# The low part of k in the attention scores, held per head in both halves of a tile

## The chip, the cores and the metric

The program runs on one core of a Trainium2 chip. A core has TensorE (PE in the profile; its weight loads are listed apart as PEld), VectorE (DVE), ScalarE (ACT), GpSimd (POOL), and SyncE (SP), whose queue issues nearly all the DMAs here. The metric is the device time of one execution in microseconds (us). On this kernel a measurement can tell a change of about 0.2% from none.

## The reference, cut to what matters

Two transformer blocks follow each other on one sequence of 512 tokens with 1024 features. Each has an attention with 8 heads. In block 1 a head has 64 dimensions; in block 2 a head has two score maps of 64 dimensions each, whose softmaxes are subtracted:

```
scores = jnp.einsum('bcqhd,bckhd->bhcqk', q, kb).astype(jnp.float32) * scale
scores = scores + bias[None, :, None]
probs = jax.nn.softmax(scores, axis=-1).astype(v.dtype)
...
s = jnp.einsum('bqhid,bkhid->bihqk', qblk, kn)
s = jnp.where(allowed, s + bias, neg)
p = jax.nn.softmax(s, axis=-1)
a = p[:, 0] - lam * p[:, 1]
```

Around the attentions stand the projections, a state-space mixer (block 1), a pooling mixer and gates (block 2), output projections and two feed-forwards. The score products are a small part of the matrix work, but they are all that the change touches.

## The kernel before, in words

Matrix products run on a reduced fp32 format (fp32r). To keep the accuracy, each operand is split into a high and a low part, and three products are added: high by high, high by low, low by high. In the dense products this is `mm3` (lines 168 to 170) and `mm3s` (lines 173 to 175): three products of 128 rows by 512 columns into one PSUM bank. The weights come from HBM in 172 units of 512 KB on SP's queue (line 137), are split by ACT (line 156) and DVE or POOL (line 157), and one unit feeds 24 products.

The scores use a trick, since a head has only 64 dimensions and a tile has 128 rows. `stack_q` makes for a head pair (block 1) or for the two maps of a head (block 2) two tiles, `qa` for e = 0 and `qb` for e = 1: 64 rows with the high part of q and 64 rows with its low part. `stack_k` makes `ka` and `kb` with the high part of k in both halves, so that one product of 128 rows (line 379) gives high by high and low by high at once. The missing high by low is a second product (line 382). For it there is one tile `kl`, which holds the low part of k of both heads as the subtraction leaves it: rows 0 to 63 for e = 0 and rows 64 to 127 for e = 1. So this product takes 64 rows of `qs[e]` and 64 rows of `kl`. The copies between halves are DMAs from SBUF to SBUF on SP's queue (lines 359, 360, 369, 370), 128 KB each.

`scores` runs over four blocks of 128 queries. Block i needs 256, 256, 384 and 512 key columns. For each it takes a PSUM bank of the `ax` pool (4 banks, handed out in turn) per e, and yields; then DVE takes the row maxima out of the bank (`row_max`, line 343), which frees it. Block 1 calls `scores` for one e at a time (`a1_first`), so line 379 and line 382 alternate, and a stack serves two heads. Block 2 calls it for e = 0 and 1 together (`a2_first`): two products of line 379, then two of line 382; after i = 2 it yields to dense work, and i = 3 comes one dense step later. After the scores come the exponentials (ACT, line 351), in block 2 the joining of the maps (POOL line 1250, DVE line 1251), the transposes of the probabilities on PE (line 390) and their copies (lines 394, 396).

PE's order is the order of the program: `drive` deals out dense products and side work in turn. The order on the other engines and on SP's queue is set by a scheduler at build time, from a simulation and the data's dependencies. Tiles for the stacks come from `RB`, a few tiles of its own and then the shared arena `RA`, first in, first out; `RB.room(n)` asks whether n are free before the next head's stack is made (`a2_prep`, in block 2 about 15 us ahead of the scores that need it).

Of the kernel before, what the change touches and what calls it, by code (L numbers as in the profile page):

```python
# [9 lines left out]
F32 = mybir.dt.float32  # L10
F32R = mybir.dt.float32r
I32 = mybir.dt.int32
AF = mybir.ActivationFunctionType
ALU = mybir.AluOpType
# [42 lines left out]
class Arena:  # L57
# [9 lines left out]
    def take(self, n):  # L67
        return [self.get() for _ in range(n)]
# [22 lines left out]
def mixer_kernel(ctx, tc, xT, xN, wst, wfa, wfb, wdt, wgrp, rbt, par, con, frow, out):  # L91
    nc = tc.nc
    V, S, G, PE = nc.vector, nc.scalar, nc.gpsimd, nc.tensor
# [13 lines left out]
    def ax_bank():  # L107
        return ps_ax.tile([128, T], F32, tag="ax", name="ax")
# [10 lines left out]
    def C(name):  # L119
        a, b = _CON[name]  # L120
        return con_sb[:, a:b]
# [185 lines left out]
    RA = Arena(base, 32, F32R, "r")  # L307
# [33 lines left out]
    def row_max(i, b, bias, s, mx):  # L341
        n = 128 * (i + 1)
        V.tensor_tensor_reduce(out=s[:, SOFF[i]:SOFF[i] + n], in0=b[:, 0:n],
                               in1=bias[:, (3 - i) * 128:512], scale=1.0, scalar=-3.0e38,
                               op0=ALU.add, op1=ALU.max, accum_out=mx[:, i:i + 1])

    def exp_rows(s, mx, nm, Z):
        V.tensor_scalar(out=nm, in0=mx, scalar1=-1.0, scalar2=None, op0=ALU.mult)  # L348
        for i in range(NT):
            n = 128 * (i + 1)  # L350
            S.activation(out=s[:, SOFF[i]:SOFF[i] + n], in_=s[:, SOFF[i]:SOFF[i] + n], func=AF.Exp,  # L351
                         bias=nm[:, i:i + 1], accum_out=Z[:, i:i + 1])

    def stack_q(qf, take, put, eng):
        qa, qb, ql = take(3)
        S.activation(out=qa, in_=qf, func=AF.Copy)
        S.activation(out=qb[64:128, :], in_=qf[64:128, :], func=AF.Copy)
        eng.tensor_tensor(out=ql, in0=qf, in1=qa.bitcast(F32), op=ALU.subtract)
        nc.sync.dma_start(out=qb.bitcast(F32)[0:64, :], in_=ql.bitcast(F32)[64:128, :])
        nc.sync.dma_start(out=qa.bitcast(F32)[64:128, :], in_=ql.bitcast(F32)[0:64, :])  # L360
        put(ql)
        return qa, qb

    def stack_k(kf, take, eng):
        ka, kb, kl = take(3)
        S.activation(out=ka, in_=kf, func=AF.Copy)
        S.activation(out=kb[64:128, :], in_=kf[64:128, :], func=AF.Copy)
        eng.tensor_tensor(out=kl, in0=kf, in1=ka.bitcast(F32), op=ALU.subtract)
        nc.sync.dma_start(out=kb.bitcast(F32)[0:64, :], in_=kb.bitcast(F32)[64:128, :])
        nc.sync.dma_start(out=ka.bitcast(F32)[64:128, :], in_=ka.bitcast(F32)[0:64, :])  # L370
        return (ka, kb), kl

    def scores(qs, ks, kl, heads):
        for i in range(NT):
            n = max(256, 128 * (i + 1))
            q0 = i * 128
            bs = [ax_bank() for _ in heads]
            for b, e in zip(bs, heads):
                PE.matmul(b[:, 0:n], lhsT=qs[e][:, q0:q0 + 128], rhs=ks[e][:, 0:n], start=True, stop=False)  # L379
            for b, e in zip(bs, heads):  # L380
                r0, r1 = e * 64, e * 64 + 64
                PE.matmul(b[:, 0:n], lhsT=qs[e][r0:r1, q0:q0 + 128], rhs=kl[r0:r1, 0:n], start=False, stop=True)  # L382
            yield i, bs

    def probs_T(s, arena, flip):
# [11 lines left out]
            res.append(t)  # L397
        return res

    # first block: mixer  # L400
    with ExitStack() as ph:
        fa_p = ph.enter_context(tc.tile_pool(name="m1f", bufs=1))
        s_p = ph.enter_context(tc.tile_pool(name="m1s", bufs=2))
        c_p = ph.enter_context(tc.tile_pool(name="m1c", bufs=1))
        FA = Arena(fa_p, 28, F32, "f")
        RB = Both(Arena(fa_p, 2, F32R, "fx"), RA)
        lw = {}

        nc.sync.dma_start(out=par_sb[:, 0:8], in_=par[:, 0:8])
# [242 lines left out]
        def qk_evac(m, b):  # L652
            t, kind = divmod(m, 2)
            f = FA.get()
            if kind == 0:
                V.scalar_tensor_tensor(out=f, in0=b, scalar=0.125, in1=lw["rb1"], op0=ALU.mult, op1=ALU.mult)
            else:
                V.tensor_tensor(out=f, in0=b, in1=lw["rb1"], op=ALU.mult)
            qk[t, kind] = stack_k(f, RB.take, G) if kind else stack_q(f, RB.take, RB.put, G)
            FA.put(f)  # L660
# [23 lines left out]
        def a1_first(hh):  # L684
            t, e = divmod(hh, 2)
            if (t, 1) not in qk:
                while (t, 1) not in qk:
                    yield False
                for _ in range(4):
                    yield True  # L690
            bias = FA.get()
            nc.sync.dma_start(out=bias, in_=rbt[hh])
            G.memset(bias[0:64, 448:512], -1.0e30)
            qs, (ks, kl) = qk[t, 0], qk[t, 1]
            s = s_p.tile([128, 1280], F32, tag="s", name="s")
            mx, nm, Z, rz = (sm.tile([128, NT], F32, tag=g, name=g) for g in ("mx", "nm", "Z", "rz"))
            for i, bs in scores(qs, ks, kl, (e,)):
                row_max(i, bs[0], bias, s, mx)
            FA.put(bias)
            exp_rows(s, mx, nm, Z)  # L700
            V.reciprocal(out=rz, in_=Z)
            if e == 1:
                RB.put(*qs, *ks, kl)
            at[hh] = (s, rz)
            yield True

# [33 lines left out]
        def att_side():  # L740
            while len(vt) < NT:
                yield False
            yield from pipeline3(range(H1), a1_first, a1_second, a1_third, 0)
            FA.put(*vt)
            yield True
            att_T(3)
            ready.add("att")
            yield True
# [85 lines left out]
        RA.put(*sch)  # L834
        RA.put(*scl)

    # feed forward
    def feed_forward(fh, fl, xside, w2, eps, name, done):
        with ExitStack() as ph:
            f_p = ph.enter_context(tc.tile_pool(name=name + "f", bufs=1))  # L840
# [194 lines left out]

    feed_forward(fh, fl, xside, wfa, 1e-5, "a", done1)

    # second block: mixer
    with ExitStack() as ph:
        fa_p = ph.enter_context(tc.tile_pool(name="m2f", bufs=1))  # L1040
        s_p = ph.enter_context(tc.tile_pool(name="m2s", bufs=3))
# [6 lines left out]
        r1, r2, rr, r1s = (c_p.tile([128, NT], F32, name=n) for n in ("r1", "r2", "rr", "r1s"))  # L1048
# [95 lines left out]
        vt, qkT, osl = {}, {}, {}  # L1144
# [62 lines left out]
        stk = {}  # L1207
        RB = Both(RY, RA)

        def a2_prep(hh):  # L1210
            qf, kf = qkT.pop(("q", hh)), qkT.pop(("k", hh))
            ks, kl = stack_k(kf, RB.take, V)
            qs = stack_q(qf, RB.take, RB.put, G)
            FA.put(qf, kf)
            stk[hh] = (qs, ks, kl)

        def a2_first(hh):
            if hh not in stk:
                while ("k", hh) not in qkT or ("q", hh) not in qkT or not RB.room(6):
                    yield False  # L1220
                a2_prep(hh)
                for _ in range(3):
                    yield True
            qs, ks, kl = stk.pop(hh)
            bias = FA.get()
            G.tensor_scalar(out=bias, in0=C("dist"), scalar1=-(2.0 ** -(hh + 1)), scalar2=1.0, op0=ALU.mult,
                            op1=ALU.mult)
            ss, rzs, mxs = [], [], []
            for i2 in range(2):
                ss.append(s_p.tile([128, 1280], F32, tag="s", name="s"))  # L1230
                mxs.append(sm.tile([128, NT], F32, tag="mx", name="mx"))
            for i, bs in scores(qs, ks, kl, (0, 1)):
                for i2 in range(2):
                    row_max(i, bs[i2], bias, ss[i2], mxs[i2])
                if i == 2:
                    yield True
            RB.put(*qs, *ks, kl)
            for i2 in range(2):
                nm, Z, rz = (sm.tile([128, NT], F32, tag=g, name=g) for g in ("nm", "Z", "rz"))
                exp_rows(ss[i2], mxs[i2], nm, Z)  # L1240
                V.reciprocal(out=rz, in_=Z)
                rzs.append(rz)
            FA.put(bias)
            if ("k", hh + 1) in qkT and ("q", hh + 1) in qkT and RB.room(6):
                a2_prep(hh + 1)
            V.tensor_scalar(out=rzs[1], in0=rzs[1], scalar1=lam, scalar2=None, op0=ALU.mult)
            for i in range(NT):
                n = 128 * (i + 1)
                a, b = ss[0][:, SOFF[i]:SOFF[i] + n], ss[1][:, SOFF[i]:SOFF[i] + n]
                G.tensor_scalar(out=b, in0=b, scalar1=rzs[1][:, i:i + 1], scalar2=1.0, op0=ALU.mult, op1=ALU.mult)  # L1250
                V.scalar_tensor_tensor(out=a, in0=a, scalar=rzs[0][:, i:i + 1], in1=b, op0=ALU.mult, op1=ALU.add)  # L1251
            hd[hh] = ss[0]
            yield True
# [25 lines left out]
        def att2_side():  # L1279
            yield from pipeline3(range(H2), a2_first, a2_second, a2_third, 2)  # L1280
# [214 lines left out]
```

## Time and profile before

| | us |
|---|---|
| median of 3 runs | 1467.81 (1467.41 to 1470.63) |
| span of the profiled execution, first to last instruction | 1468.4 |
| PE busy in it | 1445.3 (98%) |
| DVE busy | 1023.9 (70%) |
| ACT busy | 659.9 (45%) |
| POOL busy | 284.5 (19%) |

The profile gives of the profiled execution its span, and tells of no time around it; the span is 0.6 us over the median of the timed runs. The granted clock of PE is 0.995 of full speed on average and 1.00 in both attention stretches. Block 1's scores lie between 164 and 284 us, block 2's between 803 and 1007 us. A matmul's row in the timeline gives its start and how long it took in all; since matmuls overlap in the array, what one costs PE is the step from its start to the start of the next. `64*128` in a row is the part of the array that it uses: 64 rows by 128 columns.

### The profile page before, as it was taken

Reading aid. Unit: us, or ns where it says so; the run is one execution under the profiler, and the core shown is the slowest. Engines: PE = TensorE matmul, PEld = TensorE weight load, DVE = VectorE, ACT = ScalarE, POOL = GpSimd, SP = SyncE. Lnnn points to the kernel's source line nnn. Section 1 sums busy time; section 2 is a strip of 40 time slices with the busy share of each in tenths; the row PEclk is TensorE's granted clock in tenths of the full one; section 3 lists DMA queues with packets and bytes.
Section 4 is the critical chain, followed back from the end, with each engine's and each line's share of the span. In section 5 each row is a group of like instructions: output and inputs, shape, how many; then the busy total and the mean of one; then the engine's idle time right before and its main releaser. Section 6 shows DMA issues by size and latency. Waiting matters only on the chain.

```text
span 1468.4 us, 17898 instructions
## 1 busy us (share of the span) xinstructions
PE 1445.3 (98%) x6683; PEld 1171.2 (80%) x6683; DVE 1023.9 (70%) x1761; ACT 659.9 (45%) x1108; POOL 284.5 (19%) x264
## 2 busy tenths in 40 slices
PE   8979999999999999999999999999999999999998
PEld 5867777888888888888878778778888888888887
DVE  7885654573887867778684675767654878768676
ACT  5433433443554535345534636554323544445452
POOL 4664720000001010102163342322110000010101
PEclk9989999999999999999999999999999999999999
DMA  7211322222524142420223323222233523241401
GB/s 251 87 48 60 115 65 73 72 73 86 202 71 144 47 156 70 144 86 30 79 86 108 101 77 94 80 88 73 72 100 94 207 78 124 61 152 46 158 29 58
DMA packets 43526, 141.17 MB, mean 96 GB/s; under 512 B 5296, under 2 KB 5552, under 8 KB 43440
## 3 DMA queue, kind: packets, MB, share of 16 engines
q1 hardware_dynamic: 43440, 140.04, 29.8%
q8 instruction: 52, 0.85, 0.2%
q14 instruction: 34, 0.28, 0.1%
HBM read 131.63 MB, written 2.10 MB: 91 GB/s over the span
## 4 chain that ended last, share of the span: by engine, by line
PE 87%; DVE 7%; POOL 3%; issue 2%; ACT 1%; DMA 0%; SPq 0%; POOLq 0%; ACTq 0%; DVEq 0%
PE mm L168 13%; PE mm L169 12%; PE mm L170 12%; PE mm L173 11%; PE mm L174 11%; PE mm L175 11%; PE ax L175 2%; PE ax L174 2%; PE ax L173 2%; PE ax L379 1%; PE ax L382 1%; DVE wl L157 1%; PE ax L1263 1%; PE ax L721 1%; DVE s L1251 1%
## 5 line engine op out<-in xcount | busy, mean ns | idle before, releaser
L168 PE MATMUL mm<-r,wh 128*128 128x512 f32 x928 | 371.1, 400 | 0.0
L169 PE MATMUL mm<-r,wh 128*128 128x512 f32 x928 | 363.0, 391 | 1.2 <-DVE r L294 1.0
L170 PE MATMUL mm<-r,wl 128*128 128x512 f32 x928 | 362.8, 391 | 1.1 <-DVE wl L157 1.1
L156 ACT ACTIVATE wh<-wr 128x1024 fp32r<-128x1024 f32 (+1 forms) x173 | 182.4, 1054 | 388.3 <-PE mm L169 146.4
L157 DVE TENSOR_TENSOR wl<-wr,wh 128x1024 fp32r<-128x1024 f32 (+1 forms) x171 | 229.1, 1340 | 114.4 <-ACT wh L156 114.0
L173 PE MATMUL mm<-wh,r 128*128 128x512 f32 x512 | 207.2, 405 | 0.0
L168 PEld LDWEIGHTS mm<-r,wh 128*128 128x128 f32 x928 | 175.3, 189 | 39.8 <-issue 4.3
L169 PEld LDWEIGHTS mm<-r,wh 128*128 128x128 f32 x928 | 175.2, 189 | 39.5 <-DVE r L294 2.0
L170 PEld LDWEIGHTS mm<-r,wl 128*128 128x128 f32 x928 | 174.9, 189 | 38.6 <-DVE wl L157 1.5
L175 PE MATMUL mm<-wh,r 128*128 128x512 f32 x512 | 200.0, 391 | 0.0
L174 PE MATMUL mm<-wl,r 128*128 128x512 f32 x512 | 199.7, 390 | 0.3 <-DVE wl L157 0.3
L299 POOL TENSOR_TENSOR vl<-u,vh 128x512 fp32r<-128x512 f32 x36 | 47.8, 1328 | 758.2 <-ACT vh L298 757.8
L173 PEld LDWEIGHTS mm<-wh,r 128*128 128x128 f32 x512 | 96.2, 188 | 23.1 <-issue 4.4
L174 PEld LDWEIGHTS mm<-wl,r 128*128 128x128 f32 x512 | 96.3, 188 | 21.2 <-issue 1.9
L175 PEld LDWEIGHTS mm<-wh,r 128*128 128x128 f32 x512 | 96.1, 188 | 20.8
L298 ACT ACTIVATE vh<-u 128x512 fp32r<-128x512 f32 x100 | 63.0, 631 | 52.8 <-PE mm L175 37.7
L931 DVE TENSOR_TENSOR h<-h,mm 128x512 f32<-128x512 f32 x80 | 52.5, 680 | 20.9 <-PE mm L175 20.8
L351 ACT ACTIVATE s<-s,nm 128x128 f32<-128x128 f32 (+1 forms) x96 | 52.6, 550 | 28.1 <-DVE nm L348 28.1
L298 ACT ACTIVATE wh<-u 128x1024 fp32r<-128x1024 f32 (+1 forms) x32 | 32.3, 1008 | 63.1 <-PE mm L175 63.1
L298 ACT ACTIVATE wh<-t 128x1024 fp32r<-128x1024 f32 x32 | 34.0, 1063 | 56.1 <-PE mm L169 32.5
L299 DVE TENSOR_TENSOR wl<-u,wh 128x1024 fp32r<-128x1024 f32 (+1 forms) x32 | 38.0, 1188 | 25.8 <-ACT wh L298 25.8
L299 DVE TENSOR_TENSOR vl<-u,vh 128x512 fp32r<-128x512 f32 x64 | 43.7, 682 | 0.0
(338 smaller groups left out, 2364.7 us busy)
## 6 DMA issues: line engine op xcount, KB each, us to landing
wr<-in_wst_dram SPq DMA_DIRECT2D x171, 512.0 KB, 3.5
u<-in_wfa_dram SPq DMA_DIRECT2D x32, 512.0 KB, 4.3
u<-in_wfb_dram SPq DMA_DIRECT2D x32, 512.0 KB, 4.4
r<-r SPq DMA_DIRECT2D x28, 128.0 KB, 2.6
h<-in_xT_dram SPq DMA_DIRECT2D x8, 256.0 KB, 6.5
h<-in_xN_dram SPq DMA_DIRECT2D x8, 256.0 KB, 5.2
f<-in_rbt_dram SPq DMA_DIRECT2D x8, 256.0 KB, 2.7
gr<-gr SPq DMA_DIRECT2D x16, 128.0 KB, 2.8
```

The lines of the kernel that those rows point to most:

```text
L156: S.activation(out=hi[:, p], in_=t[:, p], func=AF.Copy)
L157: eng.tensor_tensor(out=lo[:, p], in0=t[:, p], in1=hi.bitcast(F32)[:, p], op=ALU.subtract)
L168: PE.matmul(ps, lhsT=wh, rhs=xh, start=first, stop=False)
L169: PE.matmul(ps, lhsT=wh, rhs=xl, start=False, stop=False)
L170: PE.matmul(ps, lhsT=wl, rhs=xh, start=False, stop=last)
L173: PE.matmul(ps, lhsT=xh, rhs=wh, start=first, stop=False, **kw)
L174: PE.matmul(ps, lhsT=xh, rhs=wl, start=False, stop=False, **kw)
L175: PE.matmul(ps, lhsT=xl, rhs=wh, start=False, stop=last, **kw)
L298: S.activation(out=hi, in_=src, func=AF.Copy)
L299: (eng or V).tensor_tensor(out=lo, in0=src, in1=hi.bitcast(F32), op=ALU.subtract)
L351: S.activation(out=s[:, SOFF[i]:SOFF[i] + n], in_=s[:, SOFF[i]:SOFF[i] + n], func=AF.Exp, bias=nm[:, i:i + 1], accum_out=Z[:, i:i + 1])
L931: V.tensor_tensor(out=ht(c, g), in0=ht(c, g), in1=b, op=ALU.add)
```

## The change

`stack_k` returns two low tiles, `la` for e = 0 and `lb` for e = 1, in place of `kl`. The subtraction writes all of `lb`. Three DMAs follow on SP's queue: rows 0 to 63 of `lb` are copied to both halves of `la`, then rows 64 to 127 of `lb` to its rows 0 to 63. The last of them overwrites what the first two read, so it is issued when those have landed. The second score product now takes all 128 rows of `qs[e]` and of `kl[e]`, which adds the product low by low. `RB` gets three more tiles of its own in block 1, and the room that block 2 asks for is 7 tiles, not 6.

```diff
     def stack_k(kf, take, eng):
-        ka, kb, kl = take(3)
+        ka, kb, la, lb = take(4)
         S.activation(out=ka, in_=kf, func=AF.Copy)
         S.activation(out=kb[64:128, :], in_=kf[64:128, :], func=AF.Copy)
-        eng.tensor_tensor(out=kl, in0=kf, in1=ka.bitcast(F32), op=ALU.subtract)
+        eng.tensor_tensor(out=lb, in0=kf, in1=ka.bitcast(F32), op=ALU.subtract)
         nc.sync.dma_start(out=kb.bitcast(F32)[0:64, :], in_=kb.bitcast(F32)[64:128, :])
         nc.sync.dma_start(out=ka.bitcast(F32)[64:128, :], in_=ka.bitcast(F32)[0:64, :])
-        return (ka, kb), kl
+        nc.sync.dma_start(out=la.bitcast(F32)[0:64, :], in_=lb.bitcast(F32)[0:64, :])
+        nc.sync.dma_start(out=la.bitcast(F32)[64:128, :], in_=lb.bitcast(F32)[0:64, :])
+        nc.sync.dma_start(out=lb.bitcast(F32)[0:64, :], in_=lb.bitcast(F32)[64:128, :])
+        return (ka, kb), (la, lb)
...
             for b, e in zip(bs, heads):
-                r0, r1 = e * 64, e * 64 + 64
-                PE.matmul(b[:, 0:n], lhsT=qs[e][r0:r1, q0:q0 + 128], rhs=kl[r0:r1, 0:n], start=False, stop=True)
+                PE.matmul(b[:, 0:n], lhsT=qs[e][:, q0:q0 + 128], rhs=kl[e][:, 0:n], start=False, stop=True)
...
-        RB = Both(Arena(fa_p, 2, F32R, "fx"), RA)
+        RB = Both(Arena(fa_p, 5, F32R, "fx"), RA)
...
-                RB.put(*qs, *ks, kl)
+                RB.put(*qs, *ks, *kl)
...
-                while ("k", hh) not in qkT or ("q", hh) not in qkT or not RB.room(6):
+                while ("k", hh) not in qkT or ("q", hh) not in qkT or not RB.room(7):
...
-            RB.put(*qs, *ks, kl)
+            RB.put(*qs, *ks, *kl)
...
-            if ("k", hh + 1) in qkT and ("q", hh + 1) in qkT and RB.room(6):
+            if ("k", hh + 1) in qkT and ("q", hh + 1) in qkT and RB.room(7):
```

PE's instructions and their order stay the same; only the rows that line 382 uses differ. DVE's order hardly moves. SP's queue has 37 rows more in the listing of its order. Line numbers of the changed kernel are 3 higher from line 374 on and 2 higher from line 384 on.

In block 2, SP's queue at the stack of a late head (359 and 360 copy halves of q, 369 and 370 of k's high part, 137 loads a weight unit) stands before as

```order
L137 DMA wr<-in_wst_dram 128x1024 x2
L369 DMA gr_5553<-gr_5553 64x512
L137 DMA wr<-in_wst_dram 128x1024
L359 DMA r_96<-r_92 64x512
L370 DMA gr_5552<-gr_5552 64x512
L360 DMA r_94<-r_92 64x512
L137 DMA wr<-in_wst_dram 128x1024 x2
```

and now, with 371 to 373 the three new copies, as

```order
L137 DMA wr<-in_wst_dram 128x1024 x2
L369 DMA gr_5568<-gr_5568 64x512
L359 DMA r_121<-r_94 64x512
L137 DMA wr<-in_wst_dram 128x1024
L360 DMA r_118<-r_94 64x512
L370 DMA gr_5567<-gr_5567 64x512
L371 DMA r_116<-r_109 64x512
L372 DMA r_116<-r_109 64x512
L373 DMA r_109<-r_109 64x512
L137 DMA wr<-in_wst_dram 128x1024 x2
```

The weight load between the copies now stands behind the q copy of line 359, and the two loads at the end stand behind the third new copy.

On ACT at the same kind of place (366, 367 and 356, 357 fill the stack, 351 are the exponentials, 1306 a gate) the order before is

```order
L366 ACTIVATE gr_5552<-g_5530 128x512
L367 ACTIVATE gr_5553<-g_5530 64x512
L356 ACTIVATE r_94<-g_5541 128x512
L1306 ACTIVATE g_5526<-g_5526,bhalf 128x512
L357 ACTIVATE r_96<-g_5541 64x512
L351 ACTIVATE s,Z<-s,nm 128x128
```

and now the q copy of line 357 comes behind the last exponential:

```order
L351 ACTIVATE s,Z<-s,nm 128x384
L351 ACTIVATE s,Z<-s,nm 128x512
L357 ACTIVATE r_94<-g_5556 64x512
L1269 ACTIVATE g_5549<-ax 128x512
L156 ACTIVATE wh<-wr 128x1024
```

So the next head's `qb` is filled some eight exponentials later, and the copy out of PSUM (line 1267 before, 1269 now) and the split of a weight unit have one 64-row copy more ahead of them.

## Rows read from the trace of the kernel before

**Rows 1.** The page: busy times; the clock in 40 slices; the last chain.

```profile
PE 1445.3 (98%) x6683; PEld 1171.2 (80%) x6683; DVE 1023.9 (70%) x1761; ACT 659.9 (45%) x1108; POOL 284.5 (19%) x264
...
PEclk9989999999999999999999999999999999999999
...
PE 87%; DVE 7%; POOL 3%; issue 2%; ACT 1%; DMA 0%; SPq 0%; POOLq 0%; ACTq 0%; DVEq 0%
```

**Rows 2.** Timeline of PE, one head of block 1: start, length, line, operands.

```profile
222.02 0.28 PE L379 MATMUL ax<-r,r 128*128 128x256 f32 x1
222.22 0.38 PE L382 MATMUL ax<-r,r 64*128 64x256 f32 x1
222.53 0.39 PE L379 MATMUL ax<-r,r 128*128 128x256 f32 x1
...
225.10 0.39 PE L174 MATMUL mm<-wl,r 128*128 128x512 f32 x1
225.33 0.40 PE L175 MATMUL mm<-wh,r 128*128 128x512 f32 x1
```

**Rows 3.** The same, block 2's first head, i = 0 to 2.

```profile
803.42 0.40 PE L379 MATMUL ax<-gr,r 128*128 128x256 f32 x2
803.75 0.38 PE L382 MATMUL ax<-r,r 64*128 64x256 f32 x2
804.06 0.50 PE L379 MATMUL ax<-gr,r 128*128 128x256 f32 x2
...
806.06 0.39 PE L174 MATMUL mm<-wl,r 128*128 128x512 f32 x1
```

**Rows 4.** The same in a narrower window: the second of the first pair.

```profile
803.54 0.28 PE L379 MATMUL ax<-gr,r 128*128 128x256 f32 x1
```

**Rows 5.** The same head, i = 3, to the second dense product behind it.

```profile
808.58 0.63 PE L379 MATMUL ax<-gr,r 128*128 128x512 f32 x2
...
809.90 0.40 PE L174 MATMUL mm<-wl,r 128*128 128x512 f32 x1
```

**Rows 6.** PE in a head of block 2 that waits at i = 2.

```profile
954.19 0.65 PE L379 MATMUL ax<-gr,r 128*128 128x384 f32 x2 [0.24 <-DVE mx L343]
...
955.47 0.39 PE L169 MATMUL mm<-r,wh 128*128 128x512 f32 x1
```

**Rows 7.** DVE just before that.

```profile
953.76 0.16 DVE L259 TENSOR_TENSOR rt<-rt,ry 128x4 f32<-128x4 f32 x1
953.84 0.28 DVE L343 CUSTOM_DVE_ANT_0 s<-ax,g 128x128 f32<-128x128 f32 x1
```

**Rows 8.** All waits of PE, 145 to 290 us: total, times, longest.

```profile
PE ax L615 <- DVE f L396: 0.3, 1, 0.3
```

**Rows 9.** All waits of PE, 760 to 1010 us.

```profile
PE ax L390 <- DVE s L1251: 2.2, 6, 0.6
PE ax L379 <- DVE mx L343: 1.2, 3, 0.7
```

**Rows 10.** A wait of DVE, 145 to 300 us.

```profile
DVE s L343 <- PE ax L382: 8.3, 22, 2.2
```

**Rows 11.** Timeline of SP's queue in block 2: issue, length, line.

```profile
792.12 0.55 SPq L370 DMA_DIRECT2D gr<-gr  x1
796.88 7.33 SPq L137 DMA_DIRECT2D wr<-in_wst_dram  x2
...
963.87 0.59 SPq L360 DMA_DIRECT2D r<-r  x1
970.71 6.20 SPq L137 DMA_DIRECT2D wr<-in_wst_dram  x2
```

**Rows 12.** Line 370's copies, both blocks: from issue to landing.

```profile
DMA to landing us min/median/max: 2.2/3.9/5.1
```

**Rows 13.** DVE: the end of a weight unit's split.

```profile
960.33 1.22 DVE L157 TENSOR_TENSOR wl<-wr,wh 128x1024 fp32r<-128x1024 f32 x1
```

**Rows 14.** PE: the first product that takes that unit.

```profile
966.86 0.39 PE L168 MATMUL mm<-r,wh 128*128 128x512 f32 x1
```

## The prediction

> **What bounds the kernel now.** I read the page first: PE is busy 98% of the span, its clock is granted in full in both attention stretches, and the chain that ended last lies to 87% on PE [rows 1]. So in this kernel time on PE is nearly time of the kernel. A busy PE says little of how well the time is spent, since matmuls overlap; what a product costs is the step to the next start. I then read the timeline of PE product by product where the change is, in both blocks [rows 2 to 6], and after that the waits of PE and DVE around it [rows 7 to 10].
>
> In block 1 the two score products alternate. A dense product of 512 columns takes 0.23 us from start to start (225.10 to 225.33). The first score product, 256 columns with 128 rows, starts at 222.02, the second, with 64 rows, at 222.22, the third, again 128 rows, at 222.53 [rows 2]: steps of 0.20 and 0.31 us. The narrow step for this width is also in the trace: in block 2 two 128-row products of 256 columns follow each other, at 803.42 and 803.54 [rows 3, 4], 0.12 us apart. So a change of row count, in either direction, costs some 0.1 to 0.2 us beyond the width. PE counts this as busy, so no table of waits shows it. Dense products have the same form (high, then low, into one bank) and step at 0.23, so it is the row count and not the shared bank.
>
> In block 2 the two 64-row products go together: both take 0.38 us [rows 3], as long as one alone [rows 2]. They use different halves of the array and run side by side. That concurrency is what the change gives up.
>
> **The change part by part.** PE's instructions and order stay. All 96 second products get 128 rows, so no change of row count is left around them. I take 0.12 us for a step of 256 columns [rows 3, 4], 0.23 for 512 [rows 2] and, halfway between, an estimate of 0.18 for 384.
>
> Block 1, per head, from the first score product (222.02) to the second dense one (225.10): 3.08 us [rows 2]. After: four products of 256, two of 384, two of 512, one dense, 4 x 0.12 + 2 x 0.18 + 2 x 0.23 + 0.23 = 1.53 us. That is 1.55 us a head. Three of the eight heads are followed by narrow state-space products, where the last 0.05 is not to be had; eight heads give **12.2 us**. Nothing there should take it back: PE's only wait in this stretch is 0.3 us, and not at the scores [rows 8], and DVE is the one that waits for the score products, 22 times, 8.3 us in all [rows 10].
>
> Block 2, first head, i = 0 to 2: 803.42 to 806.06, 2.64 us [rows 3]; after, eight of 256, four of 384, one dense, 8 x 0.12 + 4 x 0.18 + 0.23 = 1.91. Gain 0.73. Then i = 3: 808.58 to 809.90, 1.32 us [rows 5]; after, 5 x 0.23 = 1.15. Gain 0.17. Together 0.90 us, with the lost concurrency already in it (each pair now takes two steps).
>
> But i = 2 needs the banks of i = 0 back from DVE, and in five of the eight heads PE is at that boundary: three with a gap, 1.2 us in all [rows 9], and two where the bank came just as PE did. In the head of rows 6 DVE worked on a small normalisation until 953.8 and only then took the row maxima [rows 7]; it would do so after the change as well. There the gain before i = 2 is lost to a longer wait. What is left is from 954.19 on: 1.28 us to 955.47 [rows 6] against 0.28 for the second bank (the step that a pair of 384 takes now), 3 x 0.18 and 0.23, thus 1.05; gain 0.23, with i = 3 0.40 us. So three heads give 2.7 and five give 2.0: **4.7 us**. Bounds: all eight at 0.90 are 7.2; if in all eight the wait swallows what comes before i = 2, 3.2.
>
> The transposes of line 390, which wait for the joined maps [rows 9], come behind i = 3; there PE gets earlier by 0.17 us, and the first of its two results comes some 0.2 us earlier too, so I cost this wait at nothing. If the exponentials start earlier, since ACT's copy of line 357 no longer stands ahead of them, up to 2.2 us of it could go; if they don't, it could grow by 8 x 0.17 = 1.4. The same copy behind them delays a weight split by its length; the splits stand 5.3 us ahead of their use [rows 13, 14].
>
> The three new DMAs per stack, 12 stacks: their price is 0.5 us each of SP's queue [rows 11], and the third waits there for the landing of the first two, 2.2 to 5.1 us [rows 12]. Queued behind it are weight loads. In a late head of block 2 SP issues its last copy at 963.87 and the next load at 970.71 [rows 11]; 0.6 + 0.5 + 0.5 + 3.9 + 0.5 = 6.0 us fit in the 6.8. At 5.1 us the load is late by 0.4, which the lead of the splits covers. For the scores, the tightest is block 2's first stack: the new copies go out from 792.7, the third at some 797.5, it lands at about 801.5, and its product is due at 803.7. With 5.1 us twice it is late by 0.7 us, once. I cost all this at nothing; uncovered, each stack would cost PE about 5 us, 12 x 5 = 60.
>
> Sum: 12.2 + 4.7 = 16.9 us. The profiled execution has 1468.4 us of span, and the profile tells nothing of a time around it; it lies 0.6 us over the median, so I take the sum off the median: 1467.8 - 16.9 = **1450.9 us**. A count as a cross-check: 128 changes of row count at 0.19 us (1.55 / 8) are 24.8; the lost pairs cost 8 x (2 x 0.12 + 0.18 + 0.23) = 5.2; the five waiting heads lose 5 x 0.5 = 2.5; 17.1 is left.
>
> A rule of the skill speaks against the change. The pairs of block 2 do run side by side [rows 3]. The Trainium skill, TensorEngine Tiling (Array Packing), Theoretical Speedup, says that products of 64 rows or fewer gain up to twofold when they share the array; widening them throws that away, and by this rule alone the kernel gets slower by the price of the pairs. The same page, Key Properties, says that a change of tiling mode drains the engine, and the long steps of rows 2 are on that side. By the first alone the time is that of the slower rival below, by both it is the forecast.
>
> **The rivals.**
> *The other engines can't follow* (in block 2 altogether, in block 1 by half): the attention's chain of row maxima, exponentials and transposes binds, and PE waits where it used to change row count. For it: the waits of rows 9 and that DVE is 70% busy. Against: rows 8 and 10. Time: 1467.8 - 12.2 / 2 = 1461.7; if block 1 keeps all, 1455.6.
> *Slower: the long steps stay.* If they come from something else in these products, such as the change of bank group or of weights, nothing is given back and block 2's pairs are lost: per head 0.65 us, 1467.8 + 5.2 = 1473.0. It decides where a change of row count costs less than 5.2 / 128 = 0.04 us; the rows show 0.1 to 0.2. Against it: two 128-row products of different weights and banks step at 0.12 [rows 4].
> *Slower: the copies reach PE.* If weight loads behind the third copy come late in most stacks, 60 - 17 = 43 us more, 1511. Against it: rows 11, 13 and 14.
> *The change does nothing*, if the build kept 64-row parts: 1467.8. The order listing shows one product of full tiles each, so this is nearly out.
>
> **How the numbers follow.** The forecast has 0.80; its own range is 1446 (all heads of block 2 at full gain, and the wait of line 390 gone: 12.2 + 7.2 + 2.2 = 21.6) to 1454 (block 2 at 3.2, the wait up by 1.4). Engines that can't follow: 0.12. Slower with the pairs lost: 0.04; by the copies: 0.02; no change: 0.02. The range for 8 in 10 is 1446 to 1456; it takes in the part of the second case in which block 1 keeps its gain. A measurement of this kernel can tell 0.2%, 2.9 us, from no change. Faster: 0.80 + 0.12 = 0.92; same 0.02; slower 0.06.
>
> **What would show it.** Right: in the changed profile the score products of block 1 step at 0.12, 0.18 and 0.23 us, a head takes 1.5 us to the second dense product, no product of 64 rows is left, and PE's busy time falls by about 19 us while its waits grow by 2 to 3, at i = 2 of block 2. SP's queue shows the third copy some 5 us behind the first, with weight loads behind it and no wait of line 168 or 173 for a split. Wrong: steps of 0.2 and 0.3 that stay; waits of the second product for a copy; waits of line 390 or of the dense products that are longer by microseconds.

## The result, and the profile after

The changed kernel takes 1448.99 us (median of 4 runs, 1447.92 to 1450.03), the kernel before, beside it, 1468.74 (1467.41 to 1470.63). By the medians it is 19.75 us faster; the ratio is 0.9856, with a 95% interval of 0.984 to 0.9873. Forecast were 1450.9 us, a gain of 16.9 us on 1467.8, and a range of 1446 to 1456. So the time lies in the range, and the gain is 2 to 3 us larger than the sum. A second set of runs of the same kernel gave 1449.18 against 1468.71 (0.9863, 0.984 to 0.9885).

The page of the changed kernel first, with the rows that answer to [rows 1]: busy times, the clock in 40 slices, the chain that ended last by engine.

```profile
PE 1423.2 (98%) x6683; PEld 1172.2 (81%) x6683; DVE 1019.4 (70%) x1761; ACT 660.8 (46%) x1108; POOL 276.8 (19%) x264
...
PEclk9999999999999999999999999999999999999999
...
PE 82%; DVE 9%; POOL 3%; issue 3%; DMA 1%; ACT 1%; SPq 0%; POOLq 0%; DVEq 0%; ACTq 0%
```

The same 6683 products take 22.1 us less of PE's time (1445.3 to 1423.2), and the share of busy time is 98% as before: the time that went had been booked as work of PE, not as a wait. The chain is still PE's, with 82% instead of 87%.

Next PE's timeline in one head of block 1 after the change (start, length, engine, line, operands). Line 382 is the first score product, 384 the second.

```profile
214.46 0.28 PE L382 MATMUL ax<-r,r 128*128 128x256 f32 x1
214.58 0.28 PE L384 MATMUL ax<-r,r 128*128 128x256 f32 x1
214.69 0.28 PE L382 MATMUL ax<-r,r 128*128 128x256 f32 x1
...
215.75 0.40 PE L173 MATMUL mm<-wh,r 128*128 128x512 f32 x1
215.99 0.39 PE L174 MATMUL mm<-wl,r 128*128 128x512 f32 x1
```

Where the starts in [rows 2] lay 0.20 and 0.31 us apart, they lie 0.11 to 0.13 apart, and from the first score product to the second dense one the head takes 1.53 us (214.46 to 215.99) instead of 3.08.

In block 2's first head, the place of [rows 3]:

```profile
789.28 0.40 PE L382 MATMUL ax<-gr,r 128*128 128x256 f32 x2
789.52 0.40 PE L384 MATMUL ax<-r,r 128*128 128x256 f32 x2
789.76 0.40 PE L382 MATMUL ax<-gr,r 128*128 128x256 f32 x2
...
790.23 0.62 PE L382 MATMUL ax<-gr,r 128*128 128x384 f32 x2
790.68 0.51 PE L384 MATMUL ax<-r,r 128*128 128x384 f32 x2
...
791.26 0.40 PE L174 MATMUL mm<-wl,r 128*128 128x512 f32 x1
```

The pair of second products (789.52 to the next start at 789.76) now takes two steps where it took one, and still the stretch has shrunk from 2.64 us [rows 3] to 1.98. Only at i = 2 is a trace of waiting left: from 790.23 to 790.68 are 0.45 us for two products that need 0.35 elsewhere.

All waits of PE in block 2 after the change (waiting line and tile, what it waited for: us in all, times, longest), against [rows 9]:

```profile
PE ax L382 <- DVE mx L343: 2.1, 3, 1.1
PE ax L392 <- DVE s L1253: 1.0, 2, 0.6
PE ax L1196 <- POOL g L1178: 0.6, 1, 0.6
PE ax L392 <- ACT g L396: 0.3, 1, 0.3
PE ax L1196 <- DVE g L1178: 0.2, 1, 0.2
```

The wait for the banks at i = 2 went up, from 1.2 to 2.1 us; that is the forecast direction, but less than the 2 to 3 us more that the prediction named. The wait of the transposes for the joined maps (line 390 before, 392 now) went down, from 2.2 to 1.0, which the sum did not have. A wait of other transposes, line 1196, is new. In block 1 PE waits as little as in [rows 8], and the wait of [rows 10], DVE for score products, has shrunk:

```profile
DVE s L343 <- PE ax L384: 4.0, 3, 1.9
```

DVE waited 22 times and 8.3 us; now it is 3 times and 4.0 us. The banks are mostly filled before DVE comes.

I laid the two traces side by side, product by product; a shift is the start of a product in the trace after, less its start in the trace before. The shift is -2.8 us already at the first score product (161.18 against 164.00), goes to -15.25 over block 1 (12.4 us), up by 1.1 at line 1196, and down by 7.0 over block 2's heads to -21.15. Of these 7.0 us, 5.1 lie in the stretches from the first score product of a head to the second dense product behind it (i = 0 to 2, and i = 3), and 1.8 at the transposes of line 392. The spans differ by 21.5 us (1446.9, 1468.4), the medians by 19.75; the part ahead of the first score is not all the change's, as shown below.

### The profile page after: what moved, and what is told of

The parts are those of the page before. It is cut to its first block, busy times and chain, and to the rows that moved or that the text cites. A ratio compares the mean times of both kernels' runs of the same rounds, so it can differ in the third digit from the quotient of the medians.

```text
span 1446.9 us, 17960 instructions
## 1 busy us (share of the span) xinstructions
PE 1423.2 (98%) x6683; PEld 1172.2 (81%) x6683; DVE 1019.4 (70%) x1761; ACT 660.8 (46%) x1108; POOL 276.8 (19%) x264
## 4 chain that ended last, share of the span: by engine, by line
PE 82%; DVE 9%; POOL 3%; issue 3%; DMA 1%; ACT 1%; SPq 0%; POOLq 0%; DVEq 0%; ACTq 0%
PE mm L168 12%; PE mm L170 12%; PE mm L169 12%; PE mm L173 10%; PE mm L174 10%; PE mm L175 10%; DVE wl L157 2%; PE ax L175 2%; PE ax L173 2%; PE ax L174 2%; DVE s L1253 1%; PE ax L723 1%; PE ax L1265 1%; PE ax L382 1%; PE ax L617 1%
## 5 line engine op out<-in xcount | busy, mean ns | idle before, releaser
L174 PEld LDWEIGHTS mm<-wl,r 128*128 128x128 f32 x512 | 96.3, 188 | 21.5 <-issue 1.9
```

The source lines that it names most:

```text
L174: PE.matmul(ps, lhsT=xh, rhs=wl, start=False, stop=False, **kw)
```

## The experiments

Each kernel is compared with runs of the kernel before from the same session.

**The wide product alone.** The kernel before, with 128 rows in the second product. It leaves out the new tiles and copies, so the 64 rows that are added hold the other head's low part of k; the work on PE is that of the change:

```diff
-                r0, r1 = e * 64, e * 64 + 64
-                PE.matmul(b[:, 0:n], lhsT=qs[e][r0:r1, q0:q0 + 128], rhs=kl[r0:r1, 0:n], start=False, stop=True)
+                PE.matmul(b[:, 0:n], lhsT=qs[e][:, q0:q0 + 128], rhs=kl[:, 0:n], start=False, stop=True)
```

> The kernel before with one edit: the second score product takes all 128 rows of the old kl, without the new tiles and copies (it adds a wrong low part from the other head; the work on PE is that of the change). If the gain is the change of row count on PE: steps of 0.12, 0.18 and 0.23 us at the scores and 1449 to 1453 us. The waits of the transposes of line 390 should stay at about 2 us if it was the new turn of the tiles, and not the faster scores, that took them away in the changed kernel. If the new copies cost PE something, this kernel is faster than the changed one by that, below 1447. If the gain came with the copies' tiles, it is near 1468.

Measured: 1452.22 against 1468.83 us, ratio 0.9887 (0.9873 to 0.9902), a gain of 16.6 us. PE's waits in block 2 (lines 379 and 389 are the first score product and the transposes):

```profile
PE ax L379 <- DVE mx L343: 2.9, 5, 1.0
PE ax L389 <- DVE s L1250: 2.4, 6, 0.6
```

The number of rows alone gives most of the gain, and about the 16.9 us of the sum. The transposes' wait stays at 2.4 us. So faster score products do not shorten it, and its fall in the changed kernel must come from the other half of the change. Line 348, of which more below, is as long here as before, 1.25 us and more in five heads.

**The copies alone.** The changed kernel with 64 rows in the second product:

```diff
-                PE.matmul(b[:, 0:n], lhsT=qs[e][:, q0:q0 + 128], rhs=kl[e][:, 0:n], start=False, stop=True)
+                r0, r1 = e * 64, e * 64 + 64
+                PE.matmul(b[:, 0:n], lhsT=qs[e][r0:r1, q0:q0 + 128], rhs=kl[e][r0:r1, 0:n], start=False, stop=True)
```

> The changed kernel with its tiles and copies, but the second score product takes its 64 rows as before. If the copies are hidden: 1466 to 1469 us, the long steps of 0.2 and 0.3 us at the scores back, and the waits of the transposes behind line 390 gone if the turn of the tiles removes them (some 2 us less), against about 1 us of a new wait at the transposes of q and k in block 2. If the copies reach PE: above 1471.

Measured: 1466.85 against 1468.83 us, ratio 0.9985 (0.9972 to 0.9998). The copies cost nothing that shows; this half is even a gain of some 2 us, with an interval from 0.3 to 4.1. Its waits in block 2 (line 393 are the transposes, 1197 those of line 1196):

```profile
PE ax L393 <- DVE s L1254: 1.0, 2, 0.6
...
PE ax L1197 <- POOL g L1179: 0.6, 1, 0.6
```

Both the shorter wait of the transposes and the new wait are here without any wide product. They come with the new tiles and copies, whatever the second product does.

**Block 1 alone.** The changed kernel, where the second product has 128 rows in block 1 only:

```diff
-                PE.matmul(b[:, 0:n], lhsT=qs[e][:, q0:q0 + 128], rhs=kl[e][:, 0:n], start=False, stop=True)
+                r0, r1 = (0, 128) if len(heads) == 1 else (e * 64, e * 64 + 64)
+                PE.matmul(b[:, 0:n], lhsT=qs[e][r0:r1, q0:q0 + 128], rhs=kl[e][r0:r1, 0:n], start=False, stop=True)
```

> The changed kernel with 128 rows in block 1's second product and 64 rows in block 2's, where the pairs run side by side. If a change of row count costs 0.19 us in both blocks and the pairs are worth 0.65 us a head: block 1 gives 12.4 us, block 2 keeps its steps, 1454 to 1457 us. If the pairs running side by side are worth more than the changes they need, this kernel is faster than the changed one, below 1448.

Measured: 1453.52 against 1468.83 us, 0.9895 (0.9878 to 0.9911). This is half a microsecond below the expected 1454. To the changed kernel's 1449.0 to 1449.2 there are 4.3 to 4.5 us: that is what 128 rows gain in block 2, the lost pairs paid. From the copies alone (1466.85) there are 13.3, with the some 2 us to either side that the interval of the copies alone leaves: that is block 1.

**Fewer changes of row count, same rows.** This one separates the rival "the long steps stay" from the theory. The kernel before, with all its 64-row products, but in block 1 a head's four 128-row products run first and then its four 64-row products:

```diff
+        if len(heads) == 1:
...
+            bs = [ax_bank() for _ in range(NT)]
+            for i in range(NT):
+                PE.matmul(bs[i][:, 0:ns[i]], lhsT=qs[e][:, i * 128:i * 128 + 128], rhs=ks[e][:, 0:ns[i]],
+                          start=True, stop=False)
+            for i in range(NT):
+                PE.matmul(bs[i][:, 0:ns[i]], lhsT=qs[e][r0:r1, i * 128:i * 128 + 128], rhs=kl[r0:r1, 0:ns[i]],
+                          start=False, stop=True)
```

> The kernel before, 64 rows, with block 1's products of a head in another order: the four of 128 rows, then the four of 64 rows, so two changes of row count a head and not eight. If the change of row count is what costs: 8 x 6 x 0.19 = 9 us less, 1458 to 1461, with steps of 0.12, 0.18 and 0.23 us inside each group. If a 64-row product is slow by itself (0.3 us for 256 columns): near 1468, with the long steps among the 64-row products.

Measured: 1459.4 against 1468.83 us, 0.9937 (0.9922 to 0.9951), a gain of 9.4 us. PE's timeline in one head of block 1, with each group of four in one row:

```profile
216.86 0.81 PE L380 MATMUL ax<-r,r 128*128 128x256 f32 x4
217.60 0.91 PE L383 MATMUL ax<-r,r 64*128 64x256 f32 x4
218.44 0.50 PE L173 MATMUL mm<-wh,r 128*128 128x512 f32 x1
218.78 0.40 PE L174 MATMUL mm<-wl,r 128*128 128x512 f32 x1
```

The same four widths are 0.12 + 0.12 + 0.18 + 0.23 = 0.65 us without a change of row count. The wide group takes 0.74 to the next start, the narrow one 0.84, and the first dense product 0.34 instead of 0.23. So 0.09, 0.19 and 0.11 us too much, 0.39 for two changes, 0.19 for one. Looked at product by product, each change lengthens the step ahead of it and the step behind it by about 0.1 us: the last wide product takes 0.33 to the next start and the first narrow one 0.22, the last narrow one 0.33 and the first dense one 0.34. The two narrow products between step at 0.12 and 0.18, as wide ones do. With 8 changes a head there were 1.55 us to have; with 2 left there are 1.55 - 0.39 = 1.16, times 8 heads 9.3. It is the change that costs, not the 64 rows, and not the change of bank or weights, since this kernel changes the bank with every product. The Trainium skill, TensorEngine Tiling (Array Packing), Key Properties, says that a change of tiling mode drains TensorE; the trace agrees, with 0.19 us a change, and PE's busy time holds it.

**A dense step earlier.** The wait at i = 2 is the largest left in block 2. The changed kernel, with the dense step in each head of block 2 behind i = 1 instead of i = 2:

```diff
-                if i == 2:
+                if i == 1:
                     yield True
```

> The changed kernel with block 2's dense step after i = 1 of the scores and not after i = 2, so that DVE has a dense step of time to give the banks back. If the wait at i = 2 is the loss that is left: it goes, and the time falls by 2 to 3.5 us to 1445.5 to 1447. If the wait only moves, to i = 3 or to the transposes behind the exponentials, within 0.5 us of the changed kernel.

Measured: 1451.49 against 1468.71 us, 0.988 (0.9861 to 0.99), thus 2.3 us slower than the changed kernel. The wait at i = 2 is gone, as meant, but:

```profile
PE ax L392 <- DVE s L1253: 5.9, 10, 1.7
```

The wait moved to the transposes, and grew. DVE in one head:

```profile
940.51 2.25 DVE L157 TENSOR_TENSOR wl<-wr,wh 128x1024 fp32r<-128x1024 f32 x1
942.68 0.68 DVE L343 CUSTOM_DVE_ANT_0 s<-ax,g 128x512 f32<-128x512 f32 x1
```

and POOL beside it:

```profile
940.38 1.29 POOL L358 TENSOR_TENSOR r<-g,r 128x512 fp32r<-128x512 f32 x1 [1.57 <-PE ax L384]
```

PE has the first product of i = 3 at 939.45 there, right behind i = 2. DVE takes the split of a weight unit between the two, and comes to the row maxima of i = 3 at 942.68, 3.2 us behind PE's product. In the changed kernel it is 0.9 (938.47 and 939.37), with the split behind the row maxima. So the exponentials start later against PE, and the transposes pay for it. The expectation was a miss. Part of the 3.2 us is not the order of DVE: the split takes 2.25 us here and 1.22 in [rows 13]. POOL's line 358, which the last score product releases, starts 0.13 us ahead of the split and lies over it. The same holds in five heads of block 2, with 2.25 to 2.33 us; how much of the loss goes back to this was not tested. It is the overlap that is looked at below.

**The copies twice.** The changed kernel, each of the three new copies issued twice:

```diff
-        nc.sync.dma_start(out=la.bitcast(F32)[0:64, :], in_=lb.bitcast(F32)[0:64, :])
-        nc.sync.dma_start(out=la.bitcast(F32)[64:128, :], in_=lb.bitcast(F32)[0:64, :])
-        nc.sync.dma_start(out=lb.bitcast(F32)[0:64, :], in_=lb.bitcast(F32)[64:128, :])
+        for _ in range(2):
+            nc.sync.dma_start(out=la.bitcast(F32)[0:64, :], in_=lb.bitcast(F32)[0:64, :])
+            nc.sync.dma_start(out=la.bitcast(F32)[64:128, :], in_=lb.bitcast(F32)[0:64, :])
+        for _ in range(2):
+            nc.sync.dma_start(out=lb.bitcast(F32)[0:64, :], in_=lb.bitcast(F32)[64:128, :])
```

> The changed kernel with each of the three new copies issued twice (the same data), so six a stack. If SP's queue has the room that the trace shows, 36 more copies are hidden too: within 1.5 us of the changed kernel. If the copies are near to reaching PE: slower by several us, with waits of dense products for a split or of the second score product for a copy.

Measured: 1450.66 against 1468.71 us, 0.9873 (0.9854 to 0.9893), about 1.5 us over the changed kernel. PE has one wait that is not there otherwise, of the second score product for a copy:

```profile
PE ax L386 <- DMA r<-r: 1.2, 3, 0.7
```

All three are in block 2, 0.2 us in the first head, 0.7 in the second, 0.4 later, at the product of `lb`, the last tile to be filled. The first stack, which the prediction called the tightest, is among them. So the copies of the change are hidden, and with twice their number the cover is just gone in three heads.

**The changed kernel again**, for the comparisons of that session:

> The changed kernel once more, beside the two below on one chip: 1448 to 1450 us, with the wait at i = 2 of block 2's scores in the five heads in which it stood before, some 3 us in all.

Measured: 1449.18 us, told above. The wait at i = 2 is 2.0 us in three places in its profile, as in the first one, and not some 3 us in five.

**The wait that went by itself.** What do the tiles have to do with the transposes? In the trace of the kernel before I looked at a head that waits. First DVE, then POOL, then ACT; line 348 turns the row maxima into the exponentials' bias, 358 makes q's low part for the next head, 351 are the exponentials.

```profile
961.46 1.25 DVE L348 TENSOR_SCALAR nm<-mx 128x4 f32<-128x4 f32 x1
```

```profile
961.00 1.69 POOL L358 TENSOR_TENSOR r<-g,r 128x512 fp32r<-128x512 f32 x1 [5.40 <-ACT r L356]
```

```profile
962.75 0.40 ACT L351 ACTIVATE s<-s,nm 128x128 f32<-128x128 f32 x1 [0.57 <-DVE nm L348]
```

An instruction on four elements a partition takes 1.25 us, and it ends when POOL's does (962.71 and 962.69). The exponentials sit behind it. It is no single case: in block 2 of the kernel before, five of line 348's 16 instructions take 1.24 to 1.26 us and one 0.67, and all six end within 0.03 us of POOL's line 358. The same head after the change, POOL, DVE and ACT:

```profile
939.41 1.30 POOL L358 TENSOR_TENSOR r<-g,r 128x512 fp32r<-128x512 f32 x1 [3.14 <-PE ax L384]
```

```profile
941.74 0.17 DVE L348 TENSOR_SCALAR nm<-mx 128x4 f32<-128x4 f32 x1
```

```profile
941.93 0.40 ACT L351 ACTIVATE s<-s,nm 128x128 f32<-128x128 f32 x1
```

POOL's subtraction is now released by the last score product instead of ACT's copy, starts 2.3 us ahead of line 348 and is over when that starts, and takes 1.30 us instead of 1.69. The Trainium skill, SBUF — State Buffer, SBUF: two separate sides, says that GpSimd and VectorE share a pair of SBUF ports, which GpSimd, or a VectorE instruction of the kinds that need the pair, holds for a whole instruction while the other waits; the trace agrees, by the two ends 0.02 us apart.

POOL's extra 0.4 us does not come from line 348. It goes with the DVE instruction ahead of that, here the split of [rows 13], which runs for 0.54 us of POOL's time. Over line 358's six overlapped instructions before, and the six of the wide product alone, the extra is always about 0.15 us less than that overlap, down to 0.03 us where the overlap is 0.17, though line 348 takes 1.27 us there. In the changed kernel only the row maxima of line 343 run beside most of it, and it takes 1.30. So the later one waits each time: POOL for the split, line 348 for POOL.

To show that this overlap makes the wait, and not ACT's copy of line 357, which the prediction had named, I took the kernel before and put line 358 on DVE in block 2:

```diff
-            qs = stack_q(qf, RB.take, RB.put, G)
+            qs = stack_q(qf, RB.take, RB.put, V)
```

> The kernel before with the subtraction that makes q's low part in block 2 (line 358) on DVE instead of POOL. Theory: the transposes of block 2 wait because this subtraction on POOL lies over DVE's small instruction of line 348, which then takes 1.25 us instead of 0.17; with POOL idle there it takes 0.2 us, and the wait of line 390 falls from 2.2 to 1 us or less. DVE has eight times 0.68 us more: 1466.5 to 1468.5. Rival: ACT's copy of line 357 ahead of the exponentials is what makes them late; then the wait of line 390 stays at 2 us or grows with DVE's load: 1468.5 to 1470.

Measured: 1467.07 against 1469.4 us, 0.9981 (0.997 to 0.9992). The wait of the transposes, and the instructions of line 348 in block 2 (number, shortest, median and longest in ns) of this kernel:

```profile
PE ax L390 <- DVE s L1251: 0.6, 2, 0.3
...
L348 DVE TENSOR_SCALAR nm<-mx x16: 159/161/163, 811.6 to 1006.0; 128x4 f32<-128x4 f32 x16
```

The same row of the kernel before, and then of the changed one:

```profile
L348 DVE TENSOR_SCALAR nm<-mx x16: 154/161/1264, 812.0 to 1009.2; 128x4 f32<-128x4 f32 x16
```

```profile
L348 DVE TENSOR_SCALAR nm<-mx x16: 152/163/166, 797.1 to 987.8; 128x4 f32<-128x4 f32 x16
```

Without POOL in the way no instruction of line 348 takes over 0.17 us, and the transposes' wait falls from 2.2 to 0.6 us, though ACT's copy of line 357 stands ahead of the exponentials as before. The other kernels agree: the wide product alone, and the own tiles alone (further on), have the long instructions and a wait of 2.4 and 2.2 us; the copies alone have no long one and a wait of 1.0. That settles the cause. The same edit on the changed kernel:

> The changed kernel with the same subtraction on DVE. Theory: here POOL's subtraction no longer lies over line 348 in most heads, so there is little to win (the wait of the transposes is 1.0 us in all), and DVE's 0.68 us a head more can lengthen the waits at i = 2: 1448 to 1450. If DVE gets it between the row maxima and the exponentials, slower: 1450 to 1453.

Measured: 1453.64 against 1469.4 us, 0.9894 (0.9879 to 0.9908), slower than the changed kernel. By the medians of the two sessions it is some 4.5 us; the one run whose mean granted clock is 0.996, as in most runs of the changed kernel, took 1451.82, 2.6 us more than 1449.18. The median is just above the 1450 to 1453 that were expected for this case. DVE in the same head:

```profile
942.00 0.69 DVE L343 CUSTOM_DVE_ANT_0 s<-ax,g 128x512 f32<-128x512 f32 x1
...
942.62 0.69 DVE L358 TENSOR_TENSOR r<-g,r 128x512 fp32r<-128x512 f32 x1
943.22 0.68 DVE L343 CUSTOM_DVE_ANT_0 s<-ax,g 128x512 f32<-128x512 f32 x1
...
950.53 0.17 DVE L1243 RECIPROCAL rz<-Z 128x4 f32<-128x4 f32 x1
```

The subtraction stands between the two row maxima of i = 3, so the second comes 0.6 us later, and in this build ACT's copy of line 357 stands between the two sets of exponentials. From the first row max to the end of the exponentials (the second line 1243) it takes 8.5 us instead of 7.1 (939.37 to 946.44), and PE's waits for line 1253 are 4.6 us in ten places. In the kernel before it ran behind both row maxima and line 348 (959.66 us), here between the row maxima.

**The waits ahead of the scores.** The shift of -2.8 us at the first score needs its own look. Block 1's state-space products wait for DVE at other places. In the kernel before:

```profile
137.41 2.00 PE L615 MATMUL ax<-f,f 128*128 128x64 f32 x16 [1.27 <-DVE f L602]
```

and in the changed kernel:

```profile
125.52 1.10 PE L617 MATMUL ax<-f,f 128*128 128x64 f32 x8 [0.27 <-DVE f L604]
...
126.96 1.10 PE L617 MATMUL ax<-f,f 128*128 128x64 f32 x8 [0.34 <-DVE f L604]
```

By the shifts that costs 0.9 us at 126 and gives 1.4 back at 137. Of the two suspects, the three more tiles of their own in block 1 and the fourth tile per stack with its copies, I tried the first alone, on the kernel before:

```diff
-        RB = Both(Arena(fa_p, 2, F32R, "fx"), RA)
+        RB = Both(Arena(fa_p, 5, F32R, "fx"), RA)
```

> The kernel before with nothing but the three more own tiles in block 1 (five, not two); stacks, copies and products as before. Read from the traces: in the kernel before PE waits 1.27 us at 137 us in front of the state-space products of line 615, in every kernel with the new tiles it waits 0.27 and 0.34 us at 125 to 127 instead. If the own tiles do that, this kernel shows the same two short waits, and in block 2 the wait of the transposes stays at about 2.2 us, since block 2 takes other tiles: 1467.5 to 1468.5. If the fourth tile per stack does it, nothing moves: 1468.7, with the 1.27 us still there. If the tiles' turn in the arena is passed on from block 1 to block 2, the transposes' wait falls to about 1.0: 1466 to 1467.

Measured: 1469.93 against 1469.4 us, 1.0007 (0.9997 to 1.0018): no gain, and above all that was expected. Line 615 waits 1.8 us in all in four places, at most 0.8, and in block 2 the wait of line 390 stays at 2.2, and line 348 is long in the same places. So the tiles' number alone gives neither. The fourth tile and its copies, or all together, are left; they were not tried apart.

Most of the rest of the -2.8 is PE's clock. Two windows, the first behind a stretch in which PE is busy for 19.4 of 28 us, the second behind the wait of 1.27 us (start and end, length, busy time and number of instructions of each engine, granted clock as a share of 2.4 GHz, DMA share and rate), before:

```profile
88.00:94.00 6.00, 6.00 (x25) 4.82 (x24) 6.00 (x7) 2.33 (x4) 4.71 (x4) 0.69 0.28 90
140.00:145.00 5.00, 5.00 (x16) 3.64 (x15) 1.07 (x3) 0.47 (x1) 1.27 (x1) 0.71 0.00 0
```

and after:

```profile
88.00:94.00 6.00, 6.00 (x30) 4.99 (x29) 6.00 (x8) 2.06 (x4) 4.71 (x4) 0.93 0.29 90
140.00:145.00 5.00, 5.00 (x24) 4.14 (x23) 1.92 (x2) 2.21 (x3) 2.89 (x2) 1.00 0.02 3
```

Values between 0.5 and 1 are a mean over the two levels, 1.2 and 2.4 GHz. The first difference is chance: the second profile of the changed kernel has 0.69 there too. The changed kernel gains 1.2 us there on the spot, but 0.9 of it goes into a wait at line 617 at 103 us, so some 0.3 us of shift are left. Another 0.3 is there from the first 14 us; its cause stays open. The second window, with the products just ahead of it, is 1.7 us. A clock near 0.71 at 140 us shows in three of the four profiles in which PE waits 1.27 us just ahead (the fourth, of the grouped kernel, has 1.00), and in none of the kernels in which it does not. How many of the timed runs had it can't be read, but each run's mean granted clock is on record. Of the 39 runs of the kernel before in the three sessions of the experiments, 19 have 0.996 or 0.997 and took 1467.5 to 1468.8 us, 14 have 0.995 and took 1469.1 to 1470.3 (the profiled execution has 0.995 too), and 6 have 0.992 and took 1473.0 to 1474.7. The eight of the changed kernel have 0.996 or 0.998 and took 1447.9 to 1450.0. So against the best group of the kernel before, median 1468.1, the change gains some 19 us, and the rest of the 19.5 to 19.75 is no more than the mix of clocks explains.

## Why the prediction was right

**What bounds the kernel.** Right. The gain was in steps that PE books as busy, and PE's busy time fell by 22.1 us against "about 19"; some of the difference is the clock of the kernel before at 140 us, during which each product is booked as longer (16 products fill the 5 us there, 24 after).

**Block 1, 12.2 us.** Right: 12.4 by the shifts, 1.55 us a head as worked out from [rows 2], and 13.3 by two medians. All eight heads gain 1.55 us; the 0.05 us that were taken off in three of them are gained too. The step of 384 columns, an estimate, measures 0.17 to 0.18.

**Block 2, 4.7 us.** Right for the score products: 4.4 by the medians (block 1 alone against the changed kernel). The split into heads holds as well. With the wide product alone, three heads gain 0.83 us (0.90 was forecast) and the five that are at the boundary of i = 2 gain 0.37 to 0.42 (0.40), 4.4 in all. The lost pairs were priced well. The heads without a listed wait take 0.1 us too long at i = 2, as the first one above. In the changed kernel it is 5.1: three of the five gain some 0.62, and as the copies alone gain 0.15 to 0.27 in the same three, the surplus comes with the tiles and copies. In the tables the waits at i = 2 grew by 0.9 us (by 1.7 with the wide product alone), and not by "2 to 3".

**The transposes, costed at nothing.** This is the step that failed, though the forecast held. Their wait fell from 2.2 to 1.0 us by the table, and PE's shift gained 1.8 us there. "Up to 2.2 could go" stood in the text, but for the wrong reason: ACT's copy of line 357 was not what the exponentials stood behind. It was line 348 behind POOL's line 358, and the part that moved was POOL's. The row for it was within reach: a 1.25 us instruction on 128x4 elements, in the same microseconds as [rows 13].

**Other work that moved.** Not foreseen: 0.8 us of new waits at line 1196, 1.1 by the shift, and the state-space waits that gave some 0.5. With 1.8 from the transposes and 0.6 from the three heads that is 1.8 us net, beside the 2.0 (0.3 to 4.1) that the copies alone measured. 16.9 and 2.0 make 18.9, against some 19 us at like clocks. That the unforeseen parts came out on the side of a gain is luck; nothing in the prediction says that they had to.

**The copies, costed at nothing.** Right, with the reason given. SP's queue in block 2's first stack:

```profile
778.09 0.60 SPq L371 DMA_DIRECT2D r<-r  x1
778.73 0.60 SPq L372 DMA_DIRECT2D r<-r  x1
781.17 0.46 SPq L373 DMA_DIRECT2D r<-r  x1
782.75 7.27 SPq L137 DMA_DIRECT2D wr<-in_wst_dram  x2
```

The third copy goes out 3.1 us behind the first here, and 3.2 to 5.6 behind it in the seven later stacks of block 2, against "some 5"; PE waits for none of them, and the waits for a weight split (line 157) are those of before. The prediction's landing of the third copy in this stack, "about 801.5", leaves out 0.5 us of issue: 792.7 + 0.5 + 0.5 + 3.9 + 0.5 + 3.9 is 802.0, which its "late by 0.7" takes in. It didn't matter: at most 3.7 us after its issue at 781.17 the third copy had landed, and its product comes at 789.52.

**The rivals.** "The other engines can't follow" fell in block 1 by DVE's waits, 22 to 3, and holds in block 2 in the five heads at the boundary of i = 2, about as costed. "The long steps stay" fell by the grouped kernel. "The copies reach PE" does not come about even with twice the copies: no weight split is later for them, three score products wait 1.2 us in all, and the kernel loses 1.5 us. What an uncovered stack would cost, 5 us in the prediction, no run shows: where the cover ran out, it was 0.2 to 0.7 us.

## What to carry to other kernels

Read the step from start to start, not the busy time, wherever products of different row counts follow each other. At 0.19 us a change, as measured here, it paid to widen the narrow product to all rows, and in block 1 it paid to group the products by row count, which needs no new tile. When a change adds a tile to a rotating pool, look in the new order for what moved on POOL and DVE: here a small DVE instruction stood behind a long one of POOL, and a longest time far above the median of its group gave the place away. And a wait in a chain of engines can come back elsewhere when only PE's work is shifted, as with the earlier dense step, which also released POOL's instruction into DVE's split.

## What the runs showed of the hardware that I had not expected

- A change between 64 and 128 rows costs about 0.1 us in the step ahead of it and 0.1 us in the step behind it. The rows of before, where every product is a change, don't show that one change lengthens two steps.
- DVE's line 348 on 128x4 elements takes 0.16 us, and up to 1.26 us when POOL's line 358 is under way; it then ends 0.02 us behind POOL's. POOL's own instruction takes 1.30 us alone and up to 1.71 when a DVE split or subtraction is under way at its start; line 348 does not lengthen it. A DVE split of 1.22 us takes 2.25 when POOL's line 358 starts 0.13 us ahead of it.
